# Graph attention on one core: scaling each block by itself, deciding the fallback with one flag at the end, and unpacking all windows ahead of the loop

## The chip, the cores and the metric

The kernel runs on one core of one Trainium2 chip. Times are device microseconds (us) of whole executions. A profile comes from one execution; its span, from the first to the last instruction, is some 2 us shorter than the time. In the rows, PE is TensorE (matmul), PEld its weight load, DVE is VectorE, ACT is ScalarE, POOL is GpSimd, SP is SyncE; a "q" behind the name is that engine's sequencer. L12 is line 12 of the kernel of that run, so one statement has different numbers in the two kernels.

## The reference, cut to what matters

```python
# x (4096,64), edge_index (2,50000), weight (4,64,64), att_src and att_dst (4,64)
x_proj[h] = x @ weight[h]
score[h, e] = leaky_relu(x_proj[h, src] . att_src[h] + x_proj[h, dst] . att_dst[h])   # slope 0.2
output[h, dst] = sum over the edges of dst: exp(score[h, e]) * x_proj[h, src]
output[h, dst] /= (sum over the edges of dst: exp(score[h, e]) + 1e-8)
return output as (4096, 256)
```

## The kernel before

The edges are sorted twice as keys on VectorE, first by source and then within groups by destination. Then 33 blocks of 125 destinations each are worked. GpSimd fetches the sorted keys as five windows of eight blocks each. To unpack a window means to split its keys into source and destination and store both into a table in memory ("bins"); each block later loads its part of the table as `bc`. A block then takes these steps: one-hot matrices by comparing (VectorE), gathers with them (TensorE), exp and a copy to `xs` (ScalarE), weights `wv` and products `val` (VectorE), sums over edges (TensorE), a copy to `aT` (ScalarE), the projection with the weight matrix into `pf` (TensorE), the division `res` (VectorE), and the store.

The loop scales and stores a pair of blocks every second iteration:

```python
def run(self, first=0, also={}):
    for b in range(first, ND):
        self.load(b + 4)
        self.values(b, ...)                  # val, VectorE
        self.gather(b + 1, 0)
        if b:
            self.sink.project(b - 1)         # pf, TensorE
        self.sums(b, -1)
        self.gather(b + 1, 1); self.gather(b + 1, 2)
        pair = b and b % 2 == 0
        if pair:
            self.sink.invert(b - 2, 2)       # reciprocal of two blocks
        self.onehot(b + 2, halves=(0,))
        self.weights(b + 1)                  # wv
        self.onehot(b + 2, halves=(1,))
        if pair:
            self.sink.give(b - 2, 2)         # res = pf * inv of two blocks, then their stores
        self.sums(b, 0); self.sums(b, 1)
        if b in also:
            also[b]()                        # unpacks windows 2, 3, 4 in iterations 1, 2, 3
```

`pf` lies in a PSUM pool with one buffer, for a pair of blocks. The stage between sort and loop, with my remarks:

```python
group(so2, Lent(), ws1[:], spy)          # second sort, its store, then counts and window starts
win = Windows(cst, ws2[:])               # GpSimd fetches five windows
whole(so2, we2, ...)
for c in range(len(CH)):
    blocks.onehot(0, *CH[c]); blocks.gather(0, c)
win.unpack(0, nc.sync, nc.sync)
... loads of blocks 2 to 4, weights(0), values(0), block 1 spread and its one-hots ...
blocks.sums(0, -1); blocks.gather(1, 0); blocks.sums(0, 0); blocks.gather(1, 1); blocks.gather(1, 2)
win.unpack(1, nc.sync, nc.sync)
longest(so2, Lent(), (ws1, we1), (ws2, we2))  # two transposes on TensorE, one reduction
n1, n2 = room(0, EL), room(1, L)         # two register loads on every engine
blocks.sums(0, 1); blocks.weights(1); blocks.onehot(2)
blocks.run(1, {i - 1: ... win.unpack(i) for i in range(2, NI)})
...
with tc.If((n1 > W1) | (n2 > W2)):       # fallback for long runs; not taken with this data
```

## Time and profile before

| | before |
|---|---|
| time, median of 3 runs (range) | 300.62 us (300.29 to 301.66) |
| profiled span | 294.9 us |
| time of the profiled execution | 296.82 us |
| mean granted TensorE clock | 0.859 |
| VectorE busy in the loop, 175.00 to 213.89 us | 36.97 of 38.89 us |
| TensorE busy there | 38.36 of 38.89 us |

Most of the lines of this profile stand in the prediction below. Two more views carry the argument. A group row has engine, operation, output and inputs, shapes, count, then busy time in us and the mean of one in ns, then idle time before it. This is the row of the pair scaling:

```profile
L618 DVE TENSOR_TENSOR res<-pf,inv 125x512 f32<-125x512 f32 x16 | 10.9, 682 | 0.1
```

Sixteen scalings of 512 columns take 682 ns each; the 33rd block is scaled alone. The second view lists sequencer work: the count, then shortest, median and longest in ns, then the start of the first and of the last in us.

```profile
L331 DVEq TENSOR_LOAD <-most x2: 410/478/547, 129.6 to 130.2; - x2
...
L742 PEldq COMPARE_BRANCH  x1: 3771/3771/3771, 287.7 to 287.7; - x1
```

The two register loads hold up VectorE just before the loop, and TensorE's branch at the end takes 3.77 us.

### The profile page before, as it was taken

Reading aid. Unit: us, or ns where it says so; the run is one execution under the profiler, and the core shown is the slowest. Engines: PE = TensorE matmul, PEld = TensorE weight load, DVE = VectorE, ACT = ScalarE, POOL = GpSimd, SP = SyncE. Lnnn points to the kernel's source line nnn. Section 1 sums busy time; section 2 is a strip of 40 time slices with the busy share of each in tenths; the row PEclk is TensorE's granted clock in tenths of the full one; section 3 lists DMA queues with packets and bytes.
Section 4 is the critical chain, followed back from the end, with each engine's and each line's share of the span. In section 5 each row is a group of like instructions: output and inputs, shape, how many; then the busy total and the mean of one; then the engine's idle time right before and its main releaser. Section 6 shows DMA issues by size and latency. Waiting matters only on the chain.

```text
span 294.9 us, 8453 instructions
## 1 busy us (share of the span) xinstructions
PE 202.5 (69%) x3541; PEld 193.8 (66%) x3541; DVE 260.6 (88%) x504; ACT 186.0 (63%) x361; POOL 27.6 (9%) x78
## 2 busy tenths in 40 slices
PE   0001899960000007669999999999999999999980
PEld 0000599960000005559899999999999999999980
DVE  5999999995599999679999999999999999999960
ACT  2960710040599935857778787878787778777850
POOL 7882000001100002400000000000000000000000
PEclk9999975555555555899999999999999999999996
DMA  3025000000100001295768756876578657864012
GB/s 109 0 53 109 0 2 0 0 1 37 36 0 0 0 0 40 66 392 185 242 258 307 254 185 234 292 273 197 217 289 285 197 206 282 293 203 183 8 37 59
DMA packets 13326, 40.75 MB, mean 138 GB/s; under 512 B 3120, under 2 KB 8912, under 8 KB 9312
## 3 DMA queue, kind: packets, MB, share of 16 engines
q1 hardware_dynamic: 10768, 37.91, 36.4%
q10 hardware_dynamic: 1808, 1.56, 2.3%
q0 software_dynamic: 704, 0.66, 1.0%
q8 instruction: 30, 0.49, 0.7%
q14 instruction: 16, 0.13, 0.1%
HBM read 35.08 MB, written 5.05 MB: 136 GB/s over the span
## 4 chain that ended last, share of the span: by engine, by line
PE 50%; DVE 40%; issue 3%; DMA 2%; ACT 2%; DVEq 0%; POOL 0%; POOLq 0%; ACTq 0%
PE acc L545 17%; DVE sA L210 13%; DVE sB L210 12%; PE ps L494 10%; PE pf L606 6%; PE ps L492 6%; PE ps L498 5%; PE acc L538 4%; DVE val L520 2%; DVE sB L239 1%; DVE oh L471 1%; DMA eS<-in_edge_index_dram 1%; ACT xs L502 1%; DMA raw<-gat_sorted,wi 1%; DVE sA L199 1%
## 5 line engine op out<-in xcount | busy, mean ns | idle before, releaser
L502 ACT CAST xs<-ps 128x1200 bf16<-128x1200 f32 (+1 forms) x99 | 104.0, 1051 | 0.0
L520 DVE TENSOR_TENSOR val<-xs,wv 128x4096 bf16<-128x4096 bf16 (+1 forms) x34 | 75.4, 2220 | 1.0 <-ACT xs L502 1.0
L545 PE MATMUL acc<-xs,val 128*128 128x125 bf16 x1024 | 61.8, 218 | 1.9 <-issue 1.5
L494 PE MATMUL ps<-adb,oh 128*128 128x136 bf16 x528 | 62.6, 225 | 0.0
L492 PE MATMUL ps<-xa,oh 128*128 128x72 bf16 x528 | 59.9, 198 | 2.6 <-DVE oh L471 2.2
L545 PEld LDWEIGHTS <-val 128*128 128x128 bf16 x1056 | 58.8, 98 | 2.4 <-issue 1.7
L494 PEld LDWEIGHTS <-oh 128*128 128x128 bf16 x528 | 49.8, 99 | 0.5 <-issue 0.4
L492 PEld LDWEIGHTS <-oh 128*128 128x128 bf16 x528 | 47.6, 99 | 2.9 <-DVE oh L471 2.9
L500 ACT ACTIVATE ex<-ps 128x96 bf16<-128x96 f32 (+1 forms) x99 | 25.0, 252 | 33.0 <-PE ps L498 32.9
L471 DVE TENSOR_SCALAR oh<-bc,pF 128x4096 bf16<-128x4096 bf16 (+2 forms) x37 | 42.4, 1146 | 0.3 <-ACT bc L458 0.3
L210 DVE TENSOR_TENSOR sA<-sB 128x256 f32<-128x256 f32 (+2 forms) x104 | 37.2, 399 | 1.7
L210 DVE TENSOR_TENSOR sB<-sA 128x256 f32<-128x256 f32 (+2 forms) x98 | 35.1, 399 | 1.6
L498 PE MATMUL ps<-xa,oh 128*128 128x72 bf16 x528 | 33.7, 199 | 0.0
L292 PE MATMUL cnt_ps<-sgn,sel 128*128 128x17 f32 (+1 forms) x6 | 1.7, 390 | 41.9 <-ACT sgn L284 41.9
L292 PEld LDWEIGHTS cnt_ps<-sgn,sel 128*128 128x128 f32 x6 | 1.4, 318 | 42.0 <-issue 42.0
L498 PEld LDWEIGHTS <-oh 128*128 128x128 bf16 x528 | 26.7, 100 | 0.1
L474 DVE TENSOR_SCALAR oh<-bc,pF 128x2048 bf16<-128x2048 bf16 (+2 forms) x37 | 25.5, 689 | 0.0
L395 PEld LDWEIGHTS at_ps<-uv,xT 64*128 64x128 f32 x130 | 24.8, 298 | 0.3 <-issue 0.3
L395 PE MATMUL at_ps<-uv,xT 64*128 64x4 f32 x130 | 24.9, 328 | 0.0
L606 PE MATMUL pf<-Wbd,aT 128*128 128x128 f32 x132 | 22.7, 294 | 2.7 <-ACT aT L602 0.8
L281 ACT ACTIVATE junk<-kr,nb 128x512 f32<-128x512 f32 x33 | 23.8, 722 | 1.1
L606 PEld LDWEIGHTS pf<-Wbd,aT 128*128 128x128 f32 x132 | 17.3, 191 | 4.5 <-issue 3.4
(139 smaller groups left out, 213.6 us busy)
## 6 DMA issues: line engine op xcount, KB each, us to landing
bc<-gat_bins SPq DMA_DIRECT2D x31, 1024.0 KB, 9.0
out_dram<-res SPq DMA_DIRECT2D x32, 125.0 KB
eS<-in_edge_index_dram SPq DMA_DIRECT2D x2, 195.0 KB
eD<-in_edge_index_dram ACTq DMA_DIRECT2D x2, 195.0 KB
gat_bins<-tb SPq DMA_DIRECT2D x10, 32.0 KB
gat_sorted<-sA SPq DMA_DIRECT2D x1, 256.0 KB
gat_sorted<-ki SPq DMA_DIRECT2D x1, 256.0 KB
win<-gat_sorted,wi POOLq DMA_INDIRECT x5, 2.6
```

Source lines behind the costliest of these rows:

```text
L210: V.tensor_tensor(out=av(d[:], o, [2 * h, n], [1, h]), in0=av(s[:], 0, [2 * h, n], [1, h]), in1=av(s[:], h, [2 * h, n], [1, h]), op=op)
L395: T.matmul(out=ps[:, b, :], lhsT=xT[:, b * step:b * step + P], rhs=uv[:, k, :], start=(b == 0), stop=True, skip_group_check=True)
L471: V.tensor_scalar(out=oh[:, 0:2, e], in0=bc[:, :, e], scalar1=pF[:, 0:1], scalar2=None, op0=OP.is_equal)
L474: V.tensor_scalar(out=oh[:, 2, e], in0=bc[:, 1, e], scalar1=pF[:, 1:2], scalar2=None, op0=OP.is_equal)
L492: T.matmul(out=ps[:, i, P:P + XC], lhsT=oh[:, 1, e], rhs=xa[:, 2 * t, :], start=(i % 2 == 0), stop=False, skip_group_check=True)
L494: T.matmul(out=ps[:, i, 0:S0], lhsT=oh[:, 0, e], rhs=adb[:, b, :], start=False, stop=False, skip_group_check=True)
L498: T.matmul(out=ps[:, i, P:P + XC], lhsT=oh[:, 2, t * W2:(t + 1) * W2], rhs=xa[:, 2 * t + 1, :], start=False, stop=True, skip_group_check=True)
L500: S.activation(out=av(ex[:], 2 * t0, [2, n], [2 * NT, 2 * H], [1, 2]), in_=av(ps[:], P, [PW, n], [1, 2 * H], [0, 2]), func=ACTF.Exp)
L502: S.copy(out=xs[:, t0:t0 + n, 0:P + XC], in_=ps[:, 0:n, 0:P + XC])
L520: V.tensor_tensor(out=av(val[:], h * Dout, [Dout, n], [C, NT], [1, Din]), in0=av(xs[:], S0, [0, n], [XW, NT], [1, Din]), in1=av(wv[:], h * ...
L545: T.matmul(out=self.to[k], lhsT=val[:, t, k * P:(k + 1) * P], rhs=xs[:, t, 0:BD], start=apart and t == 0, stop=(t == NT - 1), skip_group_c ...
L606: T.matmul(out=self.pf[b // 2][:, b % 2, k * P:(k + 1) * P], lhsT=self.aT[b // 2][:, b % 2, k * BD:k * BD + P], rhs=Wbd[:, k, :], start=(b ...
```

## The change

It has four parts. The scaling of each block is done by itself, so that VectorE's load is even and `pf` comes free sooner. The counting of window starts is put between the last sort steps, together with five warm-up matmuls. The flag that decides on the fallback is computed on VectorE before window 0 is unpacked, and is loaded into registers once, after the loop. Windows 1 to 4 are unpacked before the loop. Two smaller edits come with them: a copy in the unpacking of window 0 moves from ScalarE to VectorE, and `onehot(2)` is now issued ahead of `weights(1)`.

```diff
 def group(...):
+        st = Stretches(pool, counts(...)[0])
+        if between:
+            warm = pp.tile([P, L], F32, name="warm")
+            for i in range(5):
+                T.matmul(out=warm[:], lhsT=identb[:], rhs=adb[:, 0:4, 0:P], start=True, stop=True)
-        store(skey2, so.runs(ki, FINE, spy))
-        bounds(pool, cps, 8 * NI, L, off2, m8, 8, ws2, we2)
-        whole(pool, ws2, 0, 0)
+        store(skey2, so.runs(ki, FINE, [lambda keys: st.count(), *(between or (quiet, quiet)),
+                                        *(lambda keys, f=f: f() for f in st.steps(0))]))
 ...
 def unpack(...):
-            (S.copy if i == 0 else V.tensor_copy)(out=tb[:, 1, :], in_=t[:, 1, :])
+            V.tensor_copy(out=tb[:, 1, :], in_=t[:, 1, :])
 ...
 def run(...):
-                pair = b and b % 2 == 0
-                if pair:
-                    self.sink.invert(b - 2, 2)
+                if b:
+                    self.sink.invert(b - 1)
 ...
-                if pair:
-                    self.sink.give(b - 2, 2)
+                if b:
+                    self.sink.give(b - 1)
 ...
 class Finish:              # still one PSUM buffer, now for one block
-                self.pf[b // 2] = self.psf.tile([P, 2, C], F32, name="pf")
+            self.pf = self.psf.tile([P, C], F32, name="pf")
 ...
         for c in range(len(CH)):
             blocks.onehot(0, *CH[c])
             blocks.gather(0, c)
+        stretches.rest()
+        longest(so2, Lent(), (ws1, we1), (ws2, we2))
+        V.tensor_scalar(out=over[:], in0=most[:, 0:1], scalar1=float(W1), ..., op0=OP.is_gt)
+        V.scalar_tensor_tensor(out=over[:], in0=most[:, 1:2], scalar=float(W2), in1=over[:], ...)
         win.unpack(0, nc.sync, nc.sync)
 ...
-        win.unpack(1, nc.sync, nc.sync)
-        longest(so2, Lent(), (ws1, we1), (ws2, we2))
-        n1, n2 = room(0, EL), room(1, L)
+        for i in range(1, NI):
+            win.unpack(i, nc.sync, nc.sync)
         blocks.sums(0, 1)
-        blocks.weights(1)
         blocks.onehot(2)
-        blocks.run(1, {i - 1: lambda i=i: win.unpack(i, nc.sync, nc.sync) for i in range(2, NI)})
+        blocks.weights(1)
+        blocks.run(1)
+        again = nc.values_load(over[0:1, 0:1], min_val=0, max_val=1, ...)
 ...
-    with tc.If((n1 > W1) | (n2 > W2)):
+    with tc.If(again > 0):
+        n1 = room(0, EL)
```

## The prediction

> **What bounds the kernel now.** I first read the page's slices and its chain that ended last, to split the span into stages. Two sorts on VectorE (exchange steps of minimum and maximum) fill the first 113 us. Then comes a stage of about 20 us in which block 0 and block 1 are prepared, and from about 133 us a loop over 33 blocks. The lines of this fence are from the page; the digits are tenths per 7.4 us slice, the last line is the chain by engine.
>
> ```profile
> PE   0001899960000007669999999999999999999980
> DVE  5999999995599999679999999999999999999960
> ACT  2960710040599935857778787878787778777850
> PEclk9999975555555555899999999999999999999996
> ...
> PE 50%; DVE 40%; issue 3%; DMA 2%; ACT 2%; DVEq 0%; POOL 0%; POOLq 0%; ACTq 0%
> ```
>
> The chain lies on VectorE while sorting and on TensorE in the loop, with VectorE nearly as full. Second view: the busy time by stretches (length, then busy time and count of PE, weight loads, DVE, ACT, POOL, then clock). Third view: VectorE's timeline of two loop iterations.
>
> ```profile
> 175.00:213.89 38.89, 38.36 (x813) 37.87 (x809) 36.97 (x41) 30.55 (x57) 0.00 (x0) 1.00 0.70 247
> ```
>
> ```profile
> 167.09 2.28 DVE L520 TENSOR_TENSOR val<-xs,wv 128x4096 bf16<-128x4096 bf16 x1
> 169.30 0.20 DVE L611 RECIPROCAL inv<-aT 125x8 f32<-125x8 f32 x1
> 169.41 1.24 DVE L471 TENSOR_SCALAR oh<-bc,pF 128x4096 bf16<-128x4096 bf16 x1
> 171.00 0.23 DVE L512 TENSOR_TENSOR wv<-ex 128x128 bf16<-128x128 bf16 x1 [0.36 <-ACT ex L500]
> 171.15 0.75 DVE L474 TENSOR_SCALAR oh<-bc,pF 128x2048 bf16<-128x2048 bf16 x1
> 171.81 0.68 DVE L618 TENSOR_TENSOR res<-pf,inv 125x512 f32<-125x512 f32 x1
> 172.41 2.28 DVE L520 TENSOR_TENSOR val<-xs,wv 128x4096 bf16<-128x4096 bf16 x1
> ```
>
> 38.89 us are eight blocks, 4.86 us each; PE is busy 4.80 of it, DVE 4.62. But the blocks are not equal. In the PE timeline the big sums start at 165.12, 169.84 and 174.84: one block takes 4.72, the next 5.00.
>
> ```profile
> 167.63 0.69 PE L606 MATMUL pf<-Wbd,aT 128*128 128x128 f32 x4
> ...
> 172.15 0.36 PE L498 MATMUL ps<-xa,oh 128*128 128x72 bf16 x6
> 172.64 0.68 PE L606 MATMUL pf<-Wbd,aT 128*128 128x128 f32 x4
> ```
>
> In the short block the projection comes 2.51 us after the start of the sums (165.12 to 167.63), in the long one 2.80 (169.84 to 172.64). These 0.29 us are a wait for the only pf buffer: the scaling of a pair (res, 171.81 + 0.68 = 172.49) must have read it, and the projection starts 0.15 later.
>
> For the stage before the loop I read the timeline and the clock by stretches:
>
> ```profile
> 115.00:116.00 1.00, 0.00 (x0) 0.00 (x0) 0.90 (x6) 0.81 (x1) 0.00 (x0) 0.50 0.00 0
> 118.00:119.00 1.00, 1.00 (x16) 1.00 (x14) 0.21 (x3) 1.00 (x2) 0.69 (x2) 0.50 0.21 53
> 119.00:120.00 1.00, 1.00 (x17) 0.90 (x15) 0.50 (x3) 0.90 (x3) 0.89 (x1) 0.63 0.30 66
> 120.00:121.00 1.00, 0.12 (x4) 0.02 (x1) 0.23 (x1) 1.00 (x3) 0.80 (x1) 1.00 0.29 72
> ```
>
> ```profile
> 129.15 0.41 DVE L327 TENSOR_REDUCE most<-mx_ps 1x2 int32<-1x256 f32 x1 [0.36 <-PE mx_ps L326]
> 130.72 0.23 DVE L512 TENSOR_TENSOR wv<-ex 128x128 bf16<-128x128 bf16 x1 [1.16 <-ACT xs L502]
> ```
>
> TensorE runs at half clock until 119 us, and VectorE stands from 129.56 to 130.72: the chain puts two register loads there (0.55 and 0.41 us), not ScalarE.
>
> **What the Trainium skill says.** (1) "TensorE: Matmul & The Clock Gate", Part 1: the array idles at half clock and is released after a busy window of about 3.4 us; the window is free-running. The trace agrees: 0.50 through the sort, released at 119 us, 3 us after dense gathers began at 116.28. (2) "VectorE: DVE Perf Modes", the section on the TRN2 errata: each instruction pays a fixed cost, an fp32 tensor_tensor takes (N+151)/0.96 ns. The trace has 682 ns for 125x512 and 285 for 125x128 against 691 and 291 by the formula, so it agrees within 2%. (3) "DMA: Bandwidth & Descriptors", Anatomy of one DMA: about 2 us are fixed, mostly the write's receipt. The trace has one: SyncE waits 1.9 us for the first sorted store after issuing it. (4) "Runtime: NRT & Kernel Launch", Instruction fetch mechanics: a taken branch to a far target stalls on fetch. The trace agrees: the branch over the fallback takes 3.77 us on PE, at the end.
>
> **The change, part by part.**
>
> *Scaling by block.* Removed per pair: one 125x512 scaling, one 125x8 reciprocal; added: two 125x256 and two reciprocals. By a line through 682 and 285 ns a 125x256 takes 0.417 us. Starts on VectorE lie about 0.08 closer than durations, so a scaling costs 0.60 now and 0.34 then, a reciprocal 0.11. VectorE's own work per block becomes 2.20 (val) + 0.11 + 1.15 (one-hot) + 0.14 (wv) + 0.66 + 0.34 = 4.60 us, below TensorE's 4.72. The loop through both engines is wv, second one-hot, scaling, projection, gathers, ScalarE's exp, wv. Projection to wv takes 171.00 - 167.63 = 3.37; wv to projection is now 172.64 - 171.00 = 1.64 and loses 0.265 with the shorter scaling: 1.375. Together 4.745 us. So each block should take 4.74 us: the larger of 4.72, 4.60 and 4.745. Against 4.866 on average (the sums at 150.54 and 281.93, 27 blocks apart) that is 27 x 0.125 = **3.4 us** gained.
>
> *Unpacking ahead of the loop.* Three unpacks of 0.60 us leave the first three iterations and go in front. These iterations are VectorE's: val starts at 132.72 and 148.12, 15.4 us for three; at 4.72 they take 14.15, **1.2 us** gained. The price of 1.8 us is paid in front of the loop.
>
> *Counting between sort steps.* After the sort, 14 dependent small operations of 0.1 to 0.2 us stand from 113.20 to 115.70 ahead of the first one-hot. Now five lie between sort steps. The trace has a like case: with one 128x128 operation between, a step takes 0.87 instead of 0.795 us, with two 0.95. So about 0.08 each; the sort ends 0.3 later, at 113.5. The window fetch does not gain: store issue at 113.39 plus some 2.2 us makes 115.6, and POOL starts at 116.12; it moves 0.3 later with the store. The one-hots of block 0 do gain. They wait for ScalarE's copies, which end at about 113.65, 114.95 and 115.9 instead of being long done. The last one-hot ends at 116.6 instead of 118.06.
>
> *Warm-up matmuls.* Five 512-column ones at half clock, 0.43 us each by the skill's figure (estimate), fill 108.4 to 110.6, and the spreading follows at once. The busy stretch of 5 us will in most runs contain a whole window, so the gathers of block 0 run at full clock: about 0.95 instead of 1.6 us to the first exp. ScalarE's last xs copy of block 0 then ends at 119.3 instead of 121.44.
>
> *Overflow flag.* Its small operations now stand ahead of unpacking window 0: rest 1.0 us, longest 0.6, transposes and reduction 1.1, flag 0.4, from 116.6 to about 119.7. So window 0 is unpacked at 120.3, while the slow copy on ScalarE that ended at 121.64 is gone: 1.3 gained for block 1. From there VectorE is the bound: val of block 0 from 120.5 to 122.75, one-hots and one copy of block 1 to 126.5 (127.66 now), four unpacks to 128.95, one-hot of block 2 to 130.85, val of block 1 at 131.0 instead of 132.72: **1.7 us** gained. The 2.4 us for maxima and register loads (128.26 to 130.72) pay for the three unpacks.
>
> *End.* One register load per engine, about 0.4 us. The last output store needs 3.6 us to land and PE's branch 3.8, so ScalarE and SyncE hide it: **0 to 0.4 us** lost.
>
> Sum: 3.4 + 1.2 + 1.7 - 0.2 = 6.1 us. I add 0.5: the clock release at 119 in this one trace is about the earliest that dense work from 116.28 allows, other runs of the kernel before should get it up to 3.4 us later, while the warmed kernel depends on it less. Predicted: 300.6 - 6.6 = 294.0 us.
>
> **Rivals.** (a) VectorE becomes the bound: more small operations at 95% busy. For it: 36.97 of 38.89. Against: the sum 4.60. If a block took 4.86 as before, the loop's 3.4 us vanish: 297.4. (b) The flag's chain in front of unpacking eats the preparation, if TensorE is still cold and the transposes come late: about 1 us less, 295. (c) The bin stores and loads become the wait: loads of blocks 2 to 4 start at about 123.5 and need 4.7 us (the median of two in this stage), so block 2 is there at 128.2 against 128.95 needed. Little slack; a miss costs below 1 us. (d) The register load at the end is exposed by a fetch stall: up to 1 us. (e) Better than thought: the mixed loop has slack and blocks run at 4.70, another 1 us: 293.
>
> **Range and chances.** The loop's gain is good to 0.7 us, preparation to 1.2, run scatter 0.5 to 1. That gives 291.8 to 297.0. The 2% line is at 294.6, close to my number: faster 0.63, same 0.36, slower 0.01.
>
> **What would show it.** Right: equal sum-to-sum distances of 4.72 to 4.76 us in the loop and no 0.29 us gap ahead of every second projection; the first loop val at about 131; clock 1.00 by 115; no stop of VectorE for registers; the fetch of the windows still at about 116.4. Wrong: 4.8 or more per block with VectorE never idle (rival a), val of block 1 at 132 or later (b, c), or a tail after the last res longer than now, 6.2 us from 288.71 (d).

## The result, and the profile after

| | before | after |
|---|---|---|
| time, median of 4 runs (range) | 301.14 us (300.29 to 301.88) | 293.34 us (293.09 to 293.79) |
| ratio, 95% interval | | 0.9744 (0.9710 to 0.9777) |
| profiled span | 294.9 us | 291.7 us |
| mean granted clock | 0.859 | 0.862 |

The results agree with the reference in all runs. The changed kernel is faster by 7.8 us at the medians. The profiled spans differ by only 3.2 us. The times alone warn of this: the profiled execution of the kernel before took 296.82 us, 3.5 less than the fastest of its timed runs, so its profile does not stand for them. 296.82 lies among the times of this kernel on the second chip below (296.40 to 298.80) and outside those on the first (300.21 to 303.66), so another chip is as good an explanation as a lucky execution. The profiled execution of the changed kernel, 293.79, is one of its four timed runs.

First the page's slices of the changed kernel, in the same form as in the prediction (40 slices, now of 7.3 us):

```profile
PE   0001899970000027478999999999999999999990
DVE  5999999996499999698999999999999999999970
...
PEclk9999975555555558887999999999999999999998
```

The loop looks fuller. The clock rises one slice earlier than before the change, in the slice that starts at 109 us, but then does not stay up: from about 117 to 139 us it stands at 8, 8, 7, where the kernel before had 8, 9, 9. Next the busy times by stretches (from:to and length, then busy time and count of PE, weight loads, DVE, ACT, POOL, then clock, DMA share, GB/s), and VectorE's timeline of one block:

```profile
174.00:213.00 39.00, 39.00 (x838) 38.90 (x835) 38.54 (x51) 31.30 (x58) 0.00 (x0) 1.00 0.71 252
```

```profile
143.75 2.28 DVE L549 TENSOR_TENSOR val<-xs,wv 128x4096 bf16<-128x4096 bf16 x1
145.95 0.17 DVE L636 RECIPROCAL inv<-aT 125x4 f32<-125x4 f32 x1
...
148.16 0.42 DVE L644 TENSOR_TENSOR res<-pf,inv 125x256 f32<-125x256 f32 x1
148.49 2.28 DVE L549 TENSOR_TENSOR val<-xs,wv 128x4096 bf16<-128x4096 bf16 x1
```

One block takes 148.49 - 143.75 = 4.74 us, and the next one starts again 4.74 later. The scaling takes 0.42. TensorE is busy all the time and VectorE 38.54 of 39.00. TensorE's timeline shows the wait for `pf` gone:

```profile
165.14 1.93 PE L574 MATMUL acc<-xs,val 128*128 128x125 bf16 x32
167.68 0.68 PE L631 MATMUL pf<-Wbd,aT 128*128 128x128 f32 x4
169.88 1.93 PE L574 MATMUL acc<-xs,val 128*128 128x125 bf16 x32
```

The projection comes 2.54 us after the start of the sums in every block, where the kernel before alternates between 2.51 and 2.80, and the sums lie 4.74 us apart in every block. This part came as predicted.

The stage before the loop did not. These rows of the timeline stand between the sort and the first `val`; the bracket gives idle time before the instruction and what released it:

```profile
117.94 0.53 PE L347 MATMUL mx_ps<-ident,mxr 128*1 128x128 f32 x2
...
120.45 0.23 ACT L529 ACTIVATE ex<-ps 128x64 bf16<-128x64 f32 x1 [2.08 <-remote]
120.52 0.41 DVE L348 TENSOR_REDUCE most<-mx_ps 1x2 int32<-1x256 f32 x1 [2.37 <-remote]
```

The transposes on TensorE are recorded as over at 118.47. VectorE's reduction, which needs only them, starts at 120.52; ScalarE waits for a gather in the same way. "Remote" means that the profile found no instruction that released the wait. I call these **late signals**: by the trace TensorE's work is done, but those who wait for it learn of it about 2 us late. (The ends of matmuls are modelled in a trace, the signals are recorded.) The trace of the kernel before has none.

To see where time went I read the start of `val` for blocks 0, 1 and 4 in each trace, and the mean distance over the 27 blocks from 4 to 31. Two more runs of the experiments are in this table, because they are the same two kernels on other occasions; all columns are us.

| trace | `val` 0 | `val` 1 | `val` 4 | 1 to 4 | mean block | end of the last `res` to the end | late signals |
|---|---|---|---|---|---|---|---|
| before | 121.47 | 132.72 | 148.12 | 15.40 | 4.860 | 6.20 | no |
| before, again (call 1 below) | 124.50 | 136.56 | 154.36 | 17.80 | 4.861 | 6.03 | yes |
| after | 122.13 | 133.17 | 148.49 | 15.32 | 4.740 | 5.81 | yes |
| after, again (call 2 below) | 120.06 | 131.46 | 146.77 | 15.31 | 4.740 | 6.07 | no |

So the profiles of before and after, read side by side, compare an execution without late signals with one that has them. Without them on either side, the gain is 294.9 - 290.2 = 4.7 us, made of 1.26 up to `val` of block 1, 0.09 in the next three blocks, 27 x 0.120 = 3.2 in the loop, and 0.1 at the end.

### The profile page after: what moved, and what is told of

The parts are those of the page before. It is cut to its first block, busy times and chain, and to the rows that moved or that the text cites. A ratio compares the mean times of both kernels' runs of the same rounds, so it can differ in the third digit from the quotient of the medians.

```text
span 291.7 us, 8543 instructions
## 1 busy us (share of the span) xinstructions
PE 202.9 (70%) x3546; PEld 194.6 (67%) x3546; DVE 262.4 (90%) x536; ACT 185.7 (64%) x360; POOL 27.6 (9%) x78
## 3 DMA queue, kind: packets, MB, share of 16 engines
q10 hardware_dynamic: 1808, 1.56, 2.4%
## 4 chain that ended last, share of the span: by engine, by line
## 5 line engine op out<-in xcount | busy, mean ns | idle before, releaser
L407 PE MATMUL ps<-ident,wS 64*128 64x64 f32 x2 | 0.7, 350 | 28.0 <-DMA wS<-in_weight_dram 28.0
```

## The experiments

Call 1 ran on a first chip, calls 2 and 3 on a second; kernels of a call share the runs of the kernel before. That kernel's median was 301.31 us in call 1, 297.22 in call 2 and 297.48 in call 3. Times of different chips are therefore not compared as such, only ratios. Call 3 hardly ran the kernel before again: seven of the eight times for it there are those of call 2.

My theory at the start: the loop's gain is the even load and the early release of `pf`; the missing part up to the loop is lost to late signals and to a fall of the TensorE clock. Rivals: the warm-up matmuls do the harm; the flag's place does; DMA bounds the stage; or the gain comes in the end from the register loads.

**The kernel before once more (call 1).** No edit.

> The kernel before, unchanged, as a control. Its profiled run spanned 294.9 us, but its timed runs take 300.3 to 301.9 us, some 4 us more than the 296.8 us of the profiled one. Theory A (clock): in most runs TensorE's clock is released later than at 119 us, or falls back once, so the runs span about 298.5 us with a lower mean clock than 0.859, and a trace of such a run shows half clock somewhere after 120 us. Theory B (chip or harness): spans stay at about 295 us with clock 0.86, and the 4 us lie outside the span. Time expected 301 us, ratio 1.00.

Measured: 301.83 us (300.27 to 302.92), ratio 0.9979 (0.9923 to 1.0036), span 301.0, clock 0.833. So the first trace of the kernel before is not what this chip shows. ScalarE's and TensorE's timelines have:

```profile
123.53 0.23 ACT L500 ACTIVATE ex<-ps 128x64 bf16<-128x64 f32 x1 [1.88 <-remote]
...
124.72 2.72 PE L456 MATMUL ps<-tb,identb 128*128 128x256 bf16 x12 [4.54 <-ACT tb L419]
```

The last exp of block 0 starts 3.35 us after TensorE's gather for it is recorded as over (at 120.18); ScalarE stands idle for 1.88 of them. The copy of window 0 comes behind it on ScalarE, so TensorE's spreading of block 1 waits 4.54 us, until 124.72, where the first trace has 1.56, until 121.68. `val` of block 0 is 3.0 us later than in the first trace, and 6.2 us are lost by block 4, while the clock was at half until 128.5 us and again from 135.3 to 142.2.

**Only the scaling by block, on the kernel before (call 1).**

```diff
-                pair = b and b % 2 == 0
-                if pair:
-                    self.sink.invert(b - 2, 2)
+                if b:
+                    self.sink.invert(b - 1)
... give and Finish in the same way, as in the change
```

> The kernel before with only the scaling and storing by single blocks. Theory (loop): 4.74 us per block, about 3.4 us faster than before: 297.5 us, ratio 0.989. Rival (VectorE becomes the bound when unpacks share the first iterations): gain below 2 us.

Measured: 299.38 us (298.65 to 300.46), ratio 0.9923 (0.9868 to 0.9979); mean block 4.736 us.

**The change with the scaling by pairs put back (call 1).** The same edit, reversed, on the changed kernel.

> The changed kernel with scaling by pairs put back, all else changed. Theory (loop): the wait of 0.29 us before every second projection returns, a block takes 4.86 us on average instead of 4.74, 27 to 30 blocks, so 3.4 us above the changed kernel: about 296.8 us, ratio 0.986. Rival (the loop's gain comes from the unpacks being gone): blocks stay at 4.74 to 4.76, time about 293.5 us. Its trace also shows whether the stop of VectorE and ScalarE from 118.1 to 120.4 us, with TensorE's three semaphore updates late by 2.0 to 2.6 us, belongs to the kernel or to that one run.

Measured: 296.76 us (296.50 to 297.17), ratio 0.9833 (0.9785 to 0.9882). Blocks alternate between 4.41 and 5.31 us, on average 4.875. VectorE's timeline of this kernel shows a `res` ahead of a `val`, as before the change:

```profile
165.30 2.28 DVE L549 TENSOR_TENSOR val<-xs,wv 128x4096 bf16<-128x4096 bf16 x1
...
170.02 0.68 DVE L645 TENSOR_TENSOR res<-pf,inv 125x512 f32<-125x512 f32 x1
170.62 2.28 DVE L549 TENSOR_TENSOR val<-xs,wv 128x4096 bf16<-128x4096 bf16 x1
```

Here 5.32 us pass from one `val` to the next. Both directions give nearly the same loop term: 27 x (4.861 - 4.736) = 3.4 us gained on the kernel before, and 27 x (4.875 - 4.742) = 3.6 lost on the changed one, against the changed kernel without warm-up of the same call. (The 27 blocks of the run with pairs hold one long block more than short ones; an even mix would be 4.86, and the loss 3.2.) The scaling by block alone carries the loop's gain. There is one more loss in this run, at the end: from the last `res` it took 7.59 us instead of 5.81 in the changed kernel, and the register load there took 0.80 us on TensorE and 1.48 on VectorE. I come back to this below. The timed gain of the single part, 1.9 us, is smaller than its loop term; in its trace the preparation was worse: `val` of block 1 came at 137.76, against 136.56 in the trace of the kernel before in this call. One more reading bears on the clock: in the run with pairs it was at full from 128.9 us on, and the three blocks from `val` 1 to `val` 4 took 14.05 us, where the changed kernel needs 15.3.

**The change without the warm-up matmuls (call 1, and again in call 3 with five rounds).**

```diff
-        if between:
-            warm = pp.tile([P, L], F32, name="warm")
-            for i in range(5):
-                T.matmul(out=warm[:], lhsT=identb[:], rhs=adb[:, 0:4, 0:P], start=True, stop=True)
```

> The changed kernel without the five warm-up matmuls. Theory A (clock): the gathers of block 0 run at half clock again and the release comes between 119 and 123 us: 1 to 4 us slower than the changed kernel, about 295.5 us. Rival (the warm-up is useless, since the trace of the changed kernel shows the clock falling back to half at 122 us after a pause of TensorE): within 0.5 us of the changed kernel, 293.3 us.

> The changed kernel without the five warm-up matmuls, beside its control. Theory of the prediction (warm-up lets the gathers of block 0 run at full clock): 0.5 to 1.5 us slower. Rival (ScalarE's copies set the pace of block 0 and the spreading alone already releases the clock by about 115 us, as the first run without warm-up showed): within 0.5 us of the control.

Measured: 292.12 us (291.69 to 293.09), ratio 0.9670 (0.9622 to 0.9718) in call 1, and 293.21 (292.55 to 294.34), ratio 0.9867 (0.9843 to 0.9891) in call 3, where the changed kernel itself took 293.74. The matmuls do what they are for: in call 3 the clock is released at 111.3 us with them and at 119.7 without (in call 1 at 114.9 without), and `val` of block 0 starts at 120.09 instead of 121.01. In these two traces the lead is kept: `val` of block 1 comes at 132.03 and at 133.24. But the trace without them is of the slowest of its runs (294.34), and no effect on the time can be told from the scatter, so neither harm nor gain of the matmuls is shown.

**The changed kernel once more (call 2, and as the control in call 3).** No edit.

> The changed kernel, unchanged, as the control on this chip. Time about 293.3 us, ratio 0.974, blocks of 4.74 us. If the stop at 118 us is a property of the kernel, its trace shows again TensorE's signals for the third gather of block 0 and for the transposes 1 to 2.5 us late, and a clock that falls back to half for one or two spells of 3.4 us between 121 and 136 us.

> The changed kernel once more, the control for the other three on this chip. Between 291.5 and 293.5 us; block 4.74 us; the distance from val of block 1 to val of block 2 is 5.84 us, with the clock at half for 3.4 us in it.

Measured: 292.10 us (291.52 to 292.48), ratio 0.9827 (0.9796 to 0.9858), span 290.2; then 293.74 (291.49 to 294.26), ratio 0.9878 (0.9837 to 0.9919), span 290.6. On this chip the gain is 5.1 and 3.7 us by the medians, below 2%, though the interval of the first reaches over that line. Neither trace has late signals. The timeline of the first:

```profile
118.45 0.41 DVE L348 TENSOR_REDUCE most<-mx_ps 1x2 int32<-1x256 f32 x1 [0.36 <-PE mx_ps L347]
...
128.67 0.23 DVE L445 TENSOR_SCALAR t<-win 128x128 int32<-128x128 int32 x1 [0.51 <-DMA win<-gat_sorted,to]
...
131.46 2.29 DVE L549 TENSOR_TENSOR val<-xs,wv 128x4096 bf16<-128x4096 bf16 x1
...
136.16 0.23 DVE L541 TENSOR_TENSOR wv<-ex 128x128 bf16<-128x128 bf16 x1 [1.14 <-ACT ex L529]
137.30 2.28 DVE L549 TENSOR_TENSOR val<-xs,wv 128x4096 bf16<-128x4096 bf16 x1
```

VectorE now waits 0.36 us for the transposes, as before the change, and not 2.37; the reduction starts 0.03 us after their recorded end (118.42). Two other things are seen. The last unpack waits 0.51 us for the fifth window's fetch (in the first trace of the changed kernel it did not wait). And the first loop block takes 137.30 - 131.46 = 5.84 us instead of 4.74, because VectorE waits 1.14 us for exps that come late. The stretches of this trace say why:

```profile
129.00:130.00 1.00, 0.00 (x0) 0.00 (x0) 1.00 (x4) 0.00 (x0) 0.00 (x0) 1.00 1.02 410
...
133.00:134.00 1.00, 1.00 (x25) 1.00 (x24) 1.00 (x3) 0.52 (x1) 0.00 (x0) 0.50 0.75 188
```

While VectorE unpacks, TensorE has nothing to do from 127.8 to 130.6. By 131 the clock has fallen to half (the column ahead of DMA share), and it stays there for 3.4 us, in which the first gathers of the loop run at half speed. The other two traces of the changed kernel have the same fall, at 132.5 and 131.8 us, after pauses of 2.2 and 3.6 us.

**The flag's transposes and reduction later (call 2).**

```diff
-        longest(so2, Lent(), (ws1, we1), (ws2, we2))
-        ... the two operations for over
+        rows = longest_rows(so2, (ws1, we1), (ws2, we2))
         win.unpack(0, nc.sync, nc.sync)
 ... after the one-hots of block 1:
+        longest_all(Lent(), rows)
+        ... the two operations for over
```

> The changed kernel with transposes, reduction and flag moved from ahead of the unpacking of window 0 to after the one-hots of block 1. Theory (rival b of the prediction: the flag's chain holds up the unpacking): window 0 is unpacked at 119 instead of 121.2 us, TensorE can spread block 1 some 2 us earlier, val of block 1 starts at about 131.3 instead of 133.2 us: 1.5 to 2 us faster than the changed kernel, ratio about 0.968. Rival (the stop of TensorE's signals until 119.5 to 120.5 us bounds the stage, the flag's chain only waits along with it): below 0.7 us.

Measured: 294.17 us (293.40 to 294.44), ratio 0.9904 (0.9876 to 0.9932). It is 2.1 us slower than the changed kernel of the same call. The unpacking of window 0 is no longer behind the flag, but the work is only moved, and `val` of block 1 comes at 132.63 instead of 131.46. The last unpack then waited 1.23 us for its window. So rival (b) of the prediction falls on this chip, where no signal came late. On the first chip, where the flag's reduction was among what waited for late signals, this edit was not run.

**Windows 1 to 4 fetched and unpacked later (call 2).**

```diff
+        def more(self):                  # called after values(0): fetches windows 1 to 4
+            rest = self.pool.tile([P, NI - 1], I32, name="wirest")
+            V.tensor_copy(out=rest[:], in_=self.start[:, 1:NI])
+            fetch(self.pool, skey2, rest[:], W2, ..., 3)
 ...
-        for i in range(1, NI):
-            win.unpack(i, nc.sync, nc.sync)
         blocks.sums(0, 1)
         blocks.onehot(2)
         blocks.weights(1)
+        for i in range(1, NI):
+            win.unpack(i, nc.sync, nc.sync)
```

> The changed kernel with the fetches of windows 1 to 4 put off until after val of block 0, and their unpacking after the one-hot of block 2. Theory (GpSimd's fetches hold up the other engines' signals): no signal of TensorE is late between 118 and 121 us, ScalarE's third exp of block 0 starts by 118.6 us and val of block 0 by 120.6 us instead of 122.1; late signals may turn up at 124 to 130 us instead. Rival (the late signals have another cause, such as instruction fetch or the switch of the clock): they stay at 118 to 120.5 us. Time between 291 and 294 us, since later fetches can cost in their new place.

Measured: 295.62 us (295.02 to 296.34), ratio 0.9958 (0.9925 to 0.9990). The run was meant to show whether GpSimd's early fetches cause the late signals. It could not, for this chip had none in any trace. What it does show is the price of a late fetch: three unpacks wait for their windows, 2.55 us in all, and `val` of block 1 starts at 134.23, 2.8 us later than in the changed kernel.

**Only the register loads of the kernel before moved to the end (call 2).**

```diff
-        n1, n2 = room(0, EL), room(1, L)
         blocks.sums(0, 1)
 ...
         blocks.run(1, ...)
+        n1, n2 = room(0, EL), room(1, L)
```

> The kernel before with the two register loads moved from the middle to the end. Theory (the loads stop VectorE and TensorE for about 1.1 us in a stage that VectorE bounds): 1 us faster than before, ratio 0.996 to 0.997. Rival (the loads are hidden, as ScalarE's xs is awaited there anyhow): 0. Second rival (a pause of TensorE there makes its clock fall back, so their removal is worth up to 3 us).

Measured: 296.87 us (296.50 to 297.56), ratio 1.0000 (0.9969 to 1.0030). `val` of block 1 comes at 131.18 instead of 132.72, so 1.5 us are gained there (against the first trace of the kernel before). From the last `res` to the end it takes 7.46 us instead of 6.20, so 1.3 us are lost. The sequencer view shows how:

```profile
L331 PEldq TENSOR_LOAD <-most x2: 827/999/1171, 285.9 to 286.8; - x2
...
L742 PEldq COMPARE_BRANCH  x1: 3532/3532/3532, 288.4 to 288.4; - x1
```

Two loads of 0.83 and 1.17 us now stand on TensorE in front of the branch of 3.53 us. The changed kernel has a single load at this place, and in all nine traces of it and its variants that scale by block, this load took 0.50 to 0.52 us on TensorE and 0.54 or 0.55 on VectorE, and the end took 5.78 to 6.22 us, no more than in the kernel before. Against the trace of the kernel before with scaling by block alone (5.67) it is 0.1 to 0.6 longer. My first reading was that one flag instead of two numbers makes the late load free. The run with the pairs put back contradicts it: it too has one flag, and its load was slow and its end long. Both kernels with a long end load their registers last and scale by pairs. So the late load is nearly free only together with the scaling by block; why the load is slower beside a pair was not tested.

**TensorE kept busy while VectorE unpacks (call 3, five rounds).** The test of the clock theory:

```diff
         blocks.sums(0, 1)
+        idle = blocks.sink.psf.tile([P, L], F32, name="idle", tag="pf")
+        for i in range(12):
+            T.matmul(out=idle[:], lhsT=identb[:], rhs=adb[:, 0:4, 0:P], start=True, stop=True)
         blocks.onehot(2)
```

> The changed kernel with twelve idle matmuls of 512 columns put on TensorE while VectorE unpacks windows 1 to 4; nothing else changes. Theory (the pause of TensorE from 127.8 to 130.6 us lets its clock fall to half for the next 3.4 us, which makes the first loop block 1.1 us longer): the clock stays at 1.00, the first block takes 4.74 us, and the kernel is 1.1 us faster than the control. Rival (the first block is long for another reason, such as the start of the pipeline): still 5.84 us, no gain.

Measured: 291.94 us (291.63 to 292.38), ratio 0.9828 (0.9806 to 0.9850), span 289.6, clock 0.870. The timeline and one stretch:

```profile
127.25 2.75 PE L760 MATMUL idle<-adb,identb 128*128 128x512 bf16 x12
...
132.27 2.29 DVE L549 TENSOR_TENSOR val<-xs,wv 128x4096 bf16<-128x4096 bf16 x1
136.87 2.28 DVE L549 TENSOR_TENSOR val<-xs,wv 128x4096 bf16<-128x4096 bf16 x1
```

```profile
132.00:133.00 1.00, 1.00 (x20) 0.91 (x18) 0.90 (x3) 0.51 (x2) 0.00 (x0) 1.00 0.86 288
```

Twelve useless matmuls fill the pause but for 1.4 us, the clock stays at 1.00 from 111.8 to 285.9 us, past TensorE's last matmul (283.0), and the first loop block takes 4.60 us instead of 5.86 in the control. From `val` 1 to `val` 4 it is 14.10 us, where the control has 15.36. The medians differ by 1.8 us, but the spans of the two traces by only 1.0. The two intervals overlap by a little, since the control scatters widely (291.49 to 294.26, where this kernel keeps within 0.75 us). So the traces show the mechanism, while the gain in time is shown for this call only: the changed kernel itself took 292.10 in call 2 on this chip, 0.16 more than this version here. In this execution the fifth window came late, and the last unpack waited 1.87 us for it. This version has the lowest median of call 3.

**The unpacks spread through the loop (call 3, five rounds).**

```diff
-        for i in range(1, NI):
-            win.unpack(i, nc.sync, nc.sync)
 ...
-        blocks.run(1)
+        blocks.run(1, {8 * i - 6: lambda i=i: win.unpack(i, nc.sync, nc.sync) for i in range(1, NI)})
```

> The changed kernel with the unpacks of windows 1 to 4 spread in the loop, after blocks 2, 10, 18 and 26, instead of ahead of it. Theory (ahead of the loop they cost their full 2.4 us, a wait for the fifth fetch and a pause of TensorE; in the loop VectorE has 0.14 us of slack a block): val of block 1 starts at about 129 us, no fall of the clock, each unpack lengthens one block by about 0.45 us; 1.5 to 2 us faster than the control, about 290.5 us. Rival (what is saved ahead is paid in the loop in full): within 0.5 us of the control.

Measured: 294.33 us (292.69 to 295.08), ratio 0.9894 (0.9861 to 0.9928). It gains nothing over the control. Without the unpacks the one-hot of block 2 is reached early and meets its load. This row of the timeline has it:

```profile
130.27 1.28 DVE L500 TENSOR_SCALAR oh<-bc,pF 128x4096 bf16<-128x4096 bf16 x1 [3.74 <-DMA bc<-gat_bins]
```

VectorE waits 3.74 us for `bc` of block 2, so `val` of block 1 still comes only at 132.45. Three of the four blocks with an unpack take 5.34 us; the first takes 6.09, as the clock falls as before (at 133.1). On this chip DMA, not VectorE, thus sets the start of the changed kernel's loop: what VectorE saves before that point turns into a wait for a window or a load. In the changed kernel's traces with late signals (the first one and the two of call 1) no unpack waits for a window; there VectorE works without a stop from the late signals to the loop's start, but for waits below 0.5 us. In the stretches of the changed kernel's trace of call 2 that start at 129 and 131 us, the DMA share is 1.02 and 0.96, at 410 and 385 GB/s.

## Why the prediction was right or wrong

The total was right: 294.0 us predicted, 293.34 measured, faster by over 2% at 0.9744. The nearness of the number is in part luck: errors of its steps compensate, as follows, and on the second chip the same change gained 3.7 to 5.1 us instead of 7.8.

**Scaling by block: right.** Predicted 4.74 us per block and 3.4 us in all; measured 4.740 and 3.2 between traces without late signals, and confirmed in both directions by the two scaling runs. The 125x256 scaling took 0.42 us, as read off the line through two sizes. Rival (a) falls: VectorE is nearly full (38.54 of 39.00 us, 4.68 a block and not the 4.60 of the sum), but a block takes 4.74 and not 4.86. Rival (e), 4.70, falls as well. The prediction had three bounds, of 4.72, 4.60 and 4.745 us; no run separates TensorE's own work from the loop through both engines.

**Unpacking ahead of the loop: wrong.** The step "at 4.72 they take 14.15, 1.2 us gained" gave 0.09 us. The three blocks did lose their unpacks, but the first of them took 5.84 us. I had put the unpacks' price of 1.8 us on VectorE alone and had not asked what TensorE does in that time. It stands for 2.2 to 3.6 us in the three traces of the changed kernel, its clock falls, and the first gathers of the loop pay for it. With the pause filled the same three blocks take 14.10 us, which is the predicted 14.15. So the term was right for a warm TensorE, and the failed step is the missing look at the clock.

**Preparation: mis-sized.** `val` of block 1 was predicted at 131.0 and came at 131.46 in the best case, a gain of 1.26 instead of 1.7 us. In the first trace of the changed kernel it came at 133.17, past the 132 that the prediction had named as a sign of (b) or (c), but there the late signals did it. In the best case the fifth window's fetch took 0.51 us, and 1.87 in another run. This is rival (c), in a place that I had not named (I had looked at the loads of blocks 2 to 4), and its size, under 1 us, was right only for the first. In the place that I had named, block 2's load was there at 130.27 in the run with spread unpacks and not at 128.2, and the control of call 3 waited 0.23 us for it. I had treated VectorE as the bound of the stage. The runs with the flag, the fetch or the unpacks moved show that on the second chip DMA sets its end: VectorE's moved work came back as a wait each time. One term failed without harm: the counting between the sort steps was to end the sort 0.3 us later, but the sorted keys' store is issued at 113.39 in both traces, and the window fetches start at 116.12 in both.

**The end: right for this kernel.** One load of 0.51 us on TensorE is hidden or nearly so: the end is no longer than before, and 0.1 to 0.6 longer than with scaling by block alone. Rival (d), an exposed load, is what the two kernels with a late load and scaling by pairs had: 1.3 and 1.8 us longer than the kernels that they were made from.

**The 0.5 us for the clock's luck: right in direction, wrong in kind and size.** I expected other executions of the kernel before to be slower than its trace, through a later clock release. (In that trace the release is at 119.74 us, not 119.) On the first chip the one that was traced was, by 6.2 us at block 4, but late signals came first, before any fall; the clock's later release and its fall came on top. With late signals the changed kernel's block 4 is 1.7 us late (148.49 against 146.77), the old kernel's 6.2. Late signals that most timed runs of the kernel before met would thus explain why the timed gain, 7.8 us, is larger than the 4.7 of the clean traces; timed runs have no trace, so this last step is argued, not shown. On the second chip, without late signals in any of its eight traces, the changed kernel gained 5.1 and 3.7 us, and the prediction's "faster by over 2%" would not have been confirmed there. All four traces of call 1, and the first of the changed kernel, have late signals.

**Open.** I do not know what delays TensorE's signals. They fall in the time of GpSimd's window fetches (116 to 122 us), but the same fetches run on the second chip without harm, so the fetches alone do not explain it. It is also not tested why the changed kernel suffers less from them. The traces offer one candidate: in the kernel before, the copy of window 0 stands on ScalarE behind the late exp and holds up TensorE's spreading until 124.72, 3.0 us later than without late signals; in the changed kernel this copy is on VectorE, and the spreading starts at 122.04, 2.1 later (119.97). And the width of the control's scatter in call 3 is unexplained.

Of the skill's statements that the prediction used, the fixed cost of VectorE's instructions held again: the new scaling took 0.419 us on average, against the 0.417 read off the line through two sizes. The branch at the end again took 3.4 to 3.8 us on TensorE in the traces where I read it; on the other four engines it took 0.05 to 0.07, so only TensorE shows a stall. The store whose 1.9 us the prediction sets beside the DMA section was issued by SyncE and moved 256 KB, while that section is on GpSimd's transfers, so it does not test the section's figure. The clock was released after a busy stretch, as "TensorE: Matmul & The Clock Gate", Part 1, says. But the prediction left out the other direction that the same section gives: the array goes back to half clock after an idle window of about 3.4 us. The traces show that fall, and after less than that.

## What to carry to other kernels

When work is moved in front of a loop, look at what every other engine does meanwhile: pauses of 2.2 to 3.6 us on TensorE put its clock to half and cost 1.3 us here, and in one trace a dozen useless matmuls, 2.75 us in all, won it back. Before saving work on one engine in a stage, find out which wait ends the stage last; where it is a DMA, as on the second chip here, the saving comes back as a wait. And check whether the profiled execution is a typical one, by its own time against the timed runs, before two profiles are subtracted: here the spans differed by 3.2 us where the timed runs differed by 7.8.

## What the Trainium skill lacked or had wrong

- "TensorE: Matmul & The Clock Gate", Part 1, gives at least one idle window of about 3.4 us as what lets the clock fall. Here it fell after pauses of 1.6, 2.2 and 2.8 us. I counted windows of 3.41 us, the length of the shortest spells at half clock, back from each change of the clock. By the matmul records TensorE was busy for 0.49, 0.37 and 0.18 of the windows before these falls; in another trace it fell after one busy for 0.52, while others with 0.43 to 0.55 left it at full. A window need not be idle, and its busy share alone does not decide.
- No page tells of signals from TensorE that reach VectorE and ScalarE late: 1.1 to 3.4 us after the recorded end of the matmul in all four traces of one chip, none in eight traces of another, where the same reduction started 0.03 us after it.
- "DMA: Bandwidth & Descriptors", Latency and other measured facts, gives about 600 ns as the floor of a tensor load. Loads of one number into registers took 410 and 547 ns on VectorE in the kernel before (284 to 773 over all engines) and 496 to 520 on TensorE in nine traces, so mostly less than that floor, but up to 1.48 us at the end of the two kernels that scale by pairs there.
- "Runtime: NRT & Kernel Launch", Instruction fetch mechanics, says that a taken branch to a far target stalls on the fetch, but gives no size. The branch over the fallback took 3.36 to 3.79 us on TensorE in six traces; that the fetch is the cause is not shown here.
